# A fixed VectorE order for the opening of the second FFN, and whole residual rows in the projection ahead of it

## The chip, the cores and the metric

The kernel runs on one core of one Trainium2 chip. The time is device microseconds for one execution of the whole two-layer block. Before the change the median of three runs is 2317.76 us (2317.74 to 2318.29).

Engines are named as in the profile: PE is TensorE, DVE is VectorE, ACT is ScalarE, POOL is GpSimd, and SP is SyncE, which here only issues DMAs. Each engine works through its own queue in order, and an instruction that waits holds everything behind it on its engine.

## The reference

The input has 1024 positions of width 1024 in float32, and two layers. Each layer adds a mixer and then an FFN to the residual `h`, both on a normalized `h`:

```
def rms_norm(x, g, eps=EPS):
    xf = x.astype(jnp.float32)
    y = xf * lax.rsqrt(jnp.mean(xf * xf, axis=-1, keepdims=True) + eps)
    return (y * g.astype(jnp.float32)).astype(x.dtype)
...
def conv_ffn(h, w_up, conv_w, conv_b, w_down):
    a, g = jnp.split(h @ w_up, 2, axis=-1)
    a = lax.conv_general_dilated(a, conv_w, window_strides=(1,), padding=((CONV_WIDTH - 1, 0),),
                                 dimension_numbers=('NWC', 'WIO', 'NWC'), feature_group_count=D_FF) + conv_b
    return (jax.nn.gelu(a) * g) @ w_down
...
    for layer in range(DEPTH):
...
        hn = rms_norm(h, norm_mix[layer])
        if layer % 2 == 0:
            mix = even_mixer(...)
        else:
            mix = odd_mixer(...)
        h = h + mix
        h = h + conv_ffn(rms_norm(h, norm_ffn[layer]), ffn_w_up[layer], ...)
    return rms_norm(h, final_norm)
```

The odd mixer of the second layer runs differential attention (six heads) and dilated attention, puts their outputs side by side and projects them with `odd_w_out` back to width 1024. The change lies between the end of that attention and the first products of the second FFN.

## The kernel before

**Numbers and tiles.** Activations lie with the width on the 128 partitions, so `h` is eight row blocks (`kt` 0 to 7) of 128 x 1024, and each row block has two halves of 512 positions. A float32 product is three matmuls: each operand is split into a high part (a cast on ACT, `wh`, `hph`) and the rest (a subtraction on DVE, `wl`, `hpl`), and `mm3` multiplies high by high, high by low and low by high. The eight pairs of blocks `hph`/`hpl` hold the split activations of whatever is projected.

**The end of the odd mixer.** `odd_mixer` runs the heads one after the other. A head is a chain over PE, ACT and DVE: scores (`sc_c`), reductions (`nmx`) and softmax (`pt_c`, `cf`), transposes on PE (`tr_c`) with their copies (`at_c`), products with v (`av_c`), a normalization by small operations on DVE (`ssq`, `rst`), and last a transpose `tr_o` and the result `y`. The output projection is cut in two. `OUT_A` are the six blocks whose input is ready early; it is done inside `odd_mixer` (loop from L1116), eight rows in two halves, 16 products `ps_o1` of 18 matmuls, in two pairs of four rows. Its PSUM tag `mm` has two banks. Each product is added on DVE to a tile `part`, loaded from the residual in DRAM, and stored back (L1123 to L1127), all by SP's queue. `part` is 128 x 512 with two buffers of the tag `sw`. `OUT_B` are the other two blocks, done after the mixer (L1310 on): 16 products `ps_o2` of 6 matmuls.

Which half a product belongs to is seen in its inputs: in the rows of the order below, `hph_0_..` is half 0 and `hph_1_..` half 1. Where a scheduler decides, instructions of the projection are placed between those of the heads, as the buffers, banks and inputs allow. qk0 and qk1 (pool `qk_p`, two buffers each) hold the rotated q and k of a head until they are laid out anew by SP's DMAs (L849).

**The opening of the second FFN.** The class `FFN` serves both layers. For layer 1 the loads of h (L1307) are issued on SP, then for each half eight products `ps_o2`; `add` (L294) adds a product to `h`, squares it on ACT (`nsq`), sums on DVE (`nsum`, L212) and stores h on SP. `ahead` prepares first weights (`wr`, and `a` for the two early columns 2 and 3). `apply` then computes the root by `Norm.stats`: `ps_n` on PE, a chain of twelve small operations on DVE, the copy `n_rb`, and `ps_b` on PE; for half 0 it scales h (`scaled`) and splits it into the blocks b11 and b21 (`put`: cast `hph` on ACT, `hpl` on DVE). Then `up` runs seven products of blocks (`PRODUCTS`) per column of the up projection into `ps_u0` to `ps_u5`; the first two use b11 and b21, and the others need half 1 as well.

```
            for half in range(2):
                for kt in range(KT):
                    ps = ps_acc("ps_o2")
                    proj_T(ps, w, kt * P, half, ncol=S, kts=OUT_B)
                    ff.add(kt, half, ps)
                ff.ahead(half)
            for half in range(2):
                ff.apply(half)
            ff.run(after1)
```

Of the kernel before, what the change touches and what calls it, by code (L numbers as in the profile page):

```python
# [10 lines left out]
F32 = mybir.dt.float32  # L11
F32R = mybir.dt.float32r
# [52 lines left out]
def tile_block(  # L65
# [22 lines left out]
    def pool(name, **kw):  # L88
        return tc.tile_pool(name=name, reuse_waits="tile", **kw)
# [184 lines left out]
    class FFN:  # L274
        def __init__(self, layer, stack):
            self.layer = layer
            hp = stack.enter_context(pool(name=f"ffh{layer}", bufs=1))
# [8 lines left out]
            self.forms = {}  # L286
# [7 lines left out]
        def add(self, kt, half, ps):  # L294
            h = self.hT[kt][half]
            V.tensor_tensor(h, ps, h, op=ALU.add)
# [4 lines left out]
        def apply(self, half):  # L301

            self.scale, _ = self.norm.stats(half * HF)
            if half == 0:
                self.X = self.blocks("x", F32R)
                X = self.X
                self.B = {
                    "b11": ([hph[m][0] for m in range(2)], [hpl[m][0] for m in range(2)]),
                    "b21": ([hph[m + 2][0] for m in range(2)], [hpl[m + 2][0] for m in range(2)]),
                    "b22": ([hph[m + 2][1] for m in range(2)], [hpl[m + 2][1] for m in range(2)]),  # L310
                    "d": ([hph[m][1] for m in range(2)], [hpl[m][1] for m in range(2)]),
                    "e": (X[0], X[1]),
                    "t3": (X[2], X[3]),
                }
                for m in range(4):
                    self.scaled(m, 0)
                    self.put("b11" if m < 2 else "b21", m % 2, self.H[m][0])

        def scaled(self, m, half):
            for kt in (2 * m, 2 * m + 1):  # L320
                t = self.hT[kt][half]
                V.scalar_tensor_tensor(t, t, pcol(PC_FFN[self.layer] + kt), self.scale, op0=ALU.mult, op1=ALU.mult)

        def put(self, name, m, src):
            hi, lo = self.B[name]
# [243 lines left out]
        def up(self):  # L569
# [3 lines left out]
            self.banks += [ps_mx.tile([P, HF], F32, tag="mx", name=f"ps_u{i + 2}") for i in range(4)]  # L573

            both = (0, 1)
            for j in both:
                self.product(j, 1)
                self.product(j, 2)
            for j in both:
                self.forms_of(j, 1)  # L580
                self.block("d", j)
                self.product(self.early[j], 1)
                self.product(self.early[j], 2)
            for j in both:
                self.product(j, 3)
            for j in both:
# [129 lines left out]
    def out_proj(ff):  # L716
        for pair in range(2):
            ws = [get_w(w_eout, pair * 2 + i, "eout") for i in range(2)]
            for half in range(2):
                for i in range(2):  # L720
                    for n in range(2):
                        kt = (pair * 2 + i) * 2 + n
                        ps = ps_acc("ps_o")
                        proj_T(ps, ws[i], n * P, half)
                        ff.add(kt, half, ps)
                    if pair == 1 and half == 1:
                        ff.ahead(i)
                if pair == 1:
                    ff.apply(half)

# [3 lines left out]
    def odd_mixer():  # L734
        stack = ExitStack()
        with stack:
# [378 lines left out]

            for pair in range(2):  # L1116
                ws = [get_w(w_oouta, pair * 2 + i, "oouta", 1536) for i in range(2)]
                for half in range(2):
                    sl = slice(half * HF, (half + 1) * HF)
                    for n in range(4):  # L1120
                        kt = pair * 4 + n
                        part = wk.tile([P, HF], F32, tag="sw", name="part", bufs=2)
                        nc.sync.dma_start(part, h_dram[kt, :, sl])  # L1123
                        ps = ps_mm.tile([P, HF], F32, tag="mm", name="ps_o1")
                        proj_T(ps, ws[n // 2], n % 2 * P, half, kts=OUT_A)
                        V.tensor_tensor(part, ps, part, op=ALU.add)
                        nc.sync.dma_start(h_dram[kt, :, sl], part)  # L1127

# [172 lines left out]
    with ExitStack() as stack:  # L1301
# [7 lines left out]
        for half in range(2):  # L1309
            for kt in range(KT):  # L1310
                ps = ps_acc("ps_o2")
                proj_T(ps, w, kt * P, half, ncol=S, kts=OUT_B)
                ff.add(kt, half, ps)
            ff.ahead(half)
        for half in range(2):
            ff.apply(half)
        ff.run(after1)


# [80 lines left out]
```

## Time and profile before

| | |
|---|---|
| median of three runs | 2317.76 us |
| the profiled execution | 2323.59 us |
| its span | 2321.8 us |
| mean granted clock of PE | 0.994 |
| PE, DVE, ACT, POOL busy in the span | 2257.7, 1670.2, 988.8, 9.4 us |
| first projection (OUT_A) beside heads and alone | 1498.9 to 1613.0 us |
| second projection (OUT_B) | 1613.0 to 1634.7 us |
| first product of the second FFN | 1647.82 us |
| DMA queues in use | SP (q1) and ACT (q10); none of POOL |

Times within the profile count from the start of its span. A row of a group has the line, engine, operation, output and inputs, shapes and count, then busy time, the mean in ns of one, and the idle time just before with what ended it. A row of a window has its bounds, its length, the busy time of each engine with its count, then the granted clock, the share of the DMA engines and what they moved. A row of the timeline has start, duration, engine and line.

### The profile page before, as it was taken

What the parts mean: (1) busy time and instruction counts of PE and PEld (TensorE: products, weight loads), DVE (VectorE), ACT (ScalarE), POOL (GpSimd) and SP (SyncE); (2) the same over time, 40 slices, a digit from 0 to 9 for tenths busy, and PEclk for the clock granted to TensorE, in tenths of its full rate; (3) what the DMA queues carried; (4) which work ended last, traced back from release to release, by engine and by line L of the source; (5) the groups of instructions that cost most, each with busy time, mean ns of one, the idle gap of its engine ahead of it and who ended that gap; (6) DMA issues with size and microseconds to landing.
All of it is one profiled execution on the core that took longest, in us unless ns stands there. A gap on an engine that the chain in (4) does not pass through costs nothing.

```text
span 2321.8 us, 31404 instructions
## 1 busy us (share of the span) xinstructions
PE 2257.7 (97%) x11436; PEld 1900.7 (82%) x11436; DVE 1670.2 (72%) x3267; ACT 988.8 (43%) x1735; POOL 9.4 (0%) x67
## 2 busy tenths in 40 slices
PE   7999999999999999999999999999899999999997
PEld 7888878888887788898988988888678888877787
DVE  6673899787866767545335798886999788766666
ACT  6331355454543333434324445553455454543331
POOL 0000000000000000000000000000000000000000
PEclk9999999999999999999999999999899999999998
DMA  4115135343468663345544253464435343468652
GB/s 136 63 46 200 37 122 195 136 163 136 163 246 288 243 220 132 100 114 131 138 107 120 78 150 97 107 178 137 151 118 199 134 166 136 163 261 295 242 190 73
DMA packets 252155, 354.85 MB, mean 153 GB/s; under 512 B 16736, under 2 KB 172640, under 8 KB 252000
## 3 DMA queue, kind: packets, MB, share of 16 engines
q1 hardware_dynamic: 251136, 351.80, 45.9%
q8 instruction: 90, 1.47, 0.3%
q10 hardware_dynamic: 864, 1.04, 0.2%
q14 instruction: 65, 0.53, 0.1%
HBM read 214.26 MB, written 103.91 MB: 137 GB/s over the span
## 4 chain that ended last, share of the span: by engine, by line
PE 63%; DMA 15%; DVE 15%; ACT 4%; issue 3%; SPq 0%; DVEq 0%; ACTq 0%
PE ps_u L173 9%; PE ps_u L175 9%; PE ps_u L174 9%; DMA wr<-in_w_up 4%; PE ps_qk L175 3%; PE ps_qk L173 3%; PE ps_qk L174 3%; DMA wr<-in_w_dn 2%; DMA hph<-g_dram 2%; DVE wl L376 2%; PE ps_o L173 2%; PE ps_o L174 2%; PE ps_o L175 2%; PE av_c L1041 2%; PE ps_vv L174 2%
## 5 line engine op out<-in xcount | busy, mean ns | idle before, releaser
L173 PE MATMUL ps_u<-hph,wh 128*128 128x512 f32 x960 | 376.3, 393 | 5.8 <-ACT hph L184 2.2
L175 PE MATMUL ps_u<-hph,wl 128*128 128x512 f32 x960 | 374.6, 391 | 0.3 <-DVE wl L376 0.3
L174 PE MATMUL ps_u<-hpl,wh 128*128 128x512 f32 x952 | 371.7, 391 | 0.2 <-DVE hpl L185 0.2
L144 DVE TENSOR_TENSOR wl<-raw,wh 128x1024 fp32r<-128x1024 f32 (+1 forms) x74 | 88.3, 1193 | 196.0 <-ACT wh L143 195.9
L173 PEld LDWEIGHTS ps_u<-hph,wh 128*128 128x128 f32 x960 | 180.6, 188 | 49.2 <-ACT f_s L448 3.4
L175 PEld LDWEIGHTS ps_u<-hph,wl 128*128 128x128 f32 x960 | 180.8, 188 | 39.5 <-DVE wl L376 1.9
L372 ACT CAST wh<-q 128x1024 fp32r<-128x1024 f32 (+1 forms) x136 | 132.8, 976 | 185.1 <-PE ps_u L174 108.2
L174 PEld LDWEIGHTS ps_u<-hpl,wh 128*128 128x128 f32 x952 | 179.4, 188 | 38.1 <-DVE hpl L185 1.3
L376 DVE TENSOR_TENSOR wl<-q,wh 128x1024 fp32r<-128x1024 f32 (+1 forms) x136 | 153.5, 1129 | 42.8 <-ACT wh L372 41.5
L173 PE MATMUL ps_qk<-hph,wh 128*128 128x512 f32 x384 | 152.0, 396 | 0.0
L175 PE MATMUL ps_qk<-hph,wl 128*128 128x512 f32 x384 | 151.3, 394 | 0.0
L174 PE MATMUL ps_qk<-hpl,wh 128*128 128x512 f32 x384 | 151.0, 393 | 0.0
L175 PE MATMUL ps_u<-x,wl 128*128 128x512 f32 x352 | 137.3, 390 | 1.1 <-DVE wl L376 1.1
L174 PE MATMUL ps_u<-x,wh 128*128 128x512 f32 x352 | 137.2, 390 | 1.1 <-DVE x L185 1.1
L173 PE MATMUL ps_u<-x,wh 128*128 128x512 f32 x352 | 137.0, 391 | 0.0
L372 ACT CAST wh<-wr 128x1024 fp32r<-128x1024 f32 (+3 forms) x132 | 100.6, 769 | 68.0 <-PE ps_u L174 34.4
L173 PE MATMUL ps_u<-h,wh 128*128 128x512 f32 x288 | 113.7, 395 | 7.5 <-ACT wh L372 4.0
L143 ACT CAST wh<-raw 128x1024 fp32r<-128x1024 f32 (+1 forms) x74 | 76.0, 1027 | 97.4 <-PE ps_qk L174 34.4
L376 DVE TENSOR_TENSOR wl<-wr,wh 128x1024 fp32r<-128x1024 f32 (+3 forms) x132 | 114.3, 870 | 3.8 <-ACT wh L372 3.6
L174 PE MATMUL ps_u<-h,wh 128*128 128x512 f32 x288 | 112.3, 390 | 1.1 <-DVE h L185 1.1
L175 PE MATMUL ps_u<-h,wl 128*128 128x512 f32 x288 | 112.2, 390 | 0.0
L174 PE MATMUL ps_vv<-wl,hph 128*128 128x256 f32 x384 | 110.0, 286 | 0.0
(276 smaller groups left out, 5262.1 us busy)
## 6 DMA issues: line engine op xcount, KB each, us to landing
wr<-in_w_up SPq DMA_DIRECT2D x88, 512.0 KB, 4.2
g_dram<-stage SPq DMA_DIRECT2D x72, 512.0 KB, 2.6
g_dram<-h SPq DMA_DIRECT2D x70, 512.0 KB, 2.6
hpl<-g_dram SPq DMA_DIRECT2D x48, 512.0 KB, 9.8
hph<-g_dram SPq DMA_DIRECT2D x48, 512.0 KB, 9.6
h<-g_dram SPq DMA_DIRECT2D x42, 512.0 KB, 5.9
wr<-in_w_dn SPq DMA_DIRECT2D x96, 192.0 KB, 2.8
raw<-in_w_oin SPq DMA_DIRECT2D x36, 512.0 KB, 3.8
```

Source lines behind the costliest of these rows:

```text
L143: A.copy(wh, raw)
L144: V.tensor_sub(wl, raw, wh.bitcast(F32))
L173: T.matmul(ps, lh, rh, start=first, stop=False, skip_group_check=more)
L174: T.matmul(ps, lh, rl, start=False, stop=False, skip_group_check=more)
L175: T.matmul(ps, ll, rh, start=False, stop=last, skip_group_check=more)
L372: A.copy(t[0], src)
L376: V.tensor_sub(l, src, h.bitcast(F32))
L1041: T.matmul(av, at, v[:, j, :], start=(j == 0), stop=(j == i))
```

## The change

Four things are done.

1. The residual's first share (OUT_A): the four rows of a pair are loaded as whole rows of 128 x 1024 into tiles `part` that use the tags `qk0` and `qk1`, ahead of the pair's products, on SP. Each half is added in place and stored by POOL's queue. The loops run as before, halves outside, rows inside.
2. The FFN of layer 1 stores h by POOL's queue (`self.queue`), that of layer 0 by SP's still.
3. The opening of the second FFN has a DVE order written by hand (`manual_schedule` for DVE): the eight projections of half 0 with squares, the first of half 1, the early weights and the root of half 0 (`stats(0)`), then the other projections of half 1 with the blocks of half 0 (`first(m)`) between them, then all squares of half 1, and after that `stats(1)`. `apply` is cut into `stats`, `places` and `first`; layer 0 calls them in the old order.
4. In `up` of layer 1, product 1 of the columns 0, 1, 2, 3 comes first and then product 2 of the same. Before, the early columns 2 and 3 came after the block d.

```
         def add(self, kt, half, ps, norm=True):
             h = self.hT[kt][half]
             V.tensor_tensor(h, ps, h, op=ALU.add)
+            if norm:
+                self.square(kt, half)
+
+        def square(self, kt, half):
+            h = self.hT[kt][half]
             self.norm.add(half * HF, kt, h)
-            nc.sync.dma_start(h_dram[kt, :, half * HF : (half + 1) * HF], h)
...
+            self.queue.dma_start(h_dram[kt, :, half * HF : (half + 1) * HF], h)
+        def stats(self, half):
+            self.scale[half], _ = self.norm.stats(half * HF)
+        def first(self, m):
+            self.scaled(m, 0)
+            self.put("b11" if m < 2 else "b21", m % 2, self.H[m][0])
...
-            for j in both:
-                self.product(j, 1)
-                self.product(j, 2)
+            if self.layer:
+                for n in (1, 2):
+                    for j in both + self.early:
+                        self.product(j, n)
...
+                parts = [qk_p.tile([P, S], F32, tag=f"qk{n % 2}", name="part") for n in range(4)]
+                for n, part in enumerate(parts):
+                    nc.sync.dma_start(part, h_dram[pair * 4 + n])
                 for half in range(2):
-                    sl = slice(half * HF, (half + 1) * HF)
-                    for n in range(4):
-                        kt = pair * 4 + n
-                        part = wk.tile([P, HF], F32, tag="sw", name="part", bufs=2)
-                        nc.sync.dma_start(part, h_dram[kt, :, sl])
+                    for n, part in enumerate(parts):
                         ps = ps_mm.tile([P, HF], F32, tag="mm", name="ps_o1")
                         proj_T(ps, ws[n // 2], n % 2 * P, half, kts=OUT_A)
+                        part = part[:, half * HF : (half + 1) * HF]
                         V.tensor_tensor(part, ps, part, op=ALU.add)
-                        nc.sync.dma_start(h_dram[kt, :, sl], part)
+                        G.dma_start(h_dram[pair * 4 + n, :, half * HF : (half + 1) * HF], part)
...
+        ff.places()
+        def project(kt, half, norm=True):
+            ps = ps_acc("ps_o2")
+            proj_T(ps, w, kt * P, half, ncol=S, kts=OUT_B)
+            ff.add(kt, half, ps, norm)
+        with tc.manual_schedule(engines={mybir.EngineType.DVE}):
+            for kt in range(KT):
+                project(kt, 0)
+            project(0, 1, False)
+            ff.ahead(0)
+            ff.stats(0)
+            project(1, 1, False)
+            project(2, 1, False)
+            ff.first(0)
+            project(3, 1, False)
+            ff.first(1)
+            project(4, 1, False)
+            project(5, 1, False)
+            ff.ahead(1)
+            ff.first(2)
+            project(6, 1, False)
+            project(7, 1, False)
+            ff.first(3)
+            for kt in range(KT):
+                ff.square(kt, 1)
+        ff.stats(1)
         ff.run(after1)
```

**PE at the end of the next-to-last head.** In the order's rows `ps_o_14354` is a product `ps_o1` with its number; here the rows of before, at that head's `tr_o`; `ps_o_14400` is the seventh product, the third of half 1:

```order
L173 MATMUL ps_o_14400<-hph_1_83,wh 128x512
L174 MATMUL ps_o_14400<-hpl_1_91,wh 128x512
L175 MATMUL ps_o_14400<-hph_1_83,wl 128x512
L898 MATMUL sc_c<-kl_13829,qs_13825 128x256 x2
L173 MATMUL ps_o_14400<-hph_1_85,wh 128x512
L1054 MATMUL tr_o<-ident,o_sb 128x128 x2
L174 MATMUL ps_o_14400<-hpl_1_93,wh 128x512
L1054 MATMUL tr_o<-ident,o_sb 128x128 x2
```

The same place after the change; `ps_o_14331` is the fourth product, the last of half 0, and `ps_o_14352` the fifth, the first of half 1:

```order
L175 MATMUL ps_o_14331<-hph_0_84,wl 128x512
L1054 MATMUL tr_c<-ident,pt_c 128x128 x7
L1060 MATMUL av_c<-v,at_c 128x128 x7
L1054 MATMUL tr_c<-ident,pt_c 128x128 x8
L1060 MATMUL av_c<-v,at_c 128x128 x8
L916 MATMUL sc_c<-kh_13827,qs_13825 128x256
L916 MATMUL sc_c<-kh_13828,qs_13826 128x256
L917 MATMUL sc_c<-kl_13830,qs_13826 128x256
L916 MATMUL sc_c<-kh_13827,qs_13825 128x256
L1073 MATMUL tr_o<-ident,o_sb 128x128 x4
L173 MATMUL ps_o_14352<-hph_1_89,wh 128x512
```

The matmuls of three half-1 products that stood among the head's transposes and products with v are now behind its `tr_o`. Counted through the whole order, 121 matmuls of `ps_o1` stood ahead of the end of this head and 72 do now; ahead of the last `tr_o` of the last head it was 226 and is 178, of 288.

**DVE at the same place.** After the change, the end of that head's small operations, its result `y`, and the adds of the products `ps_o_14310` and `ps_o_14331`, which are rows 2 and 3 of half 0:

```order
L1069 TENSOR_SCALAR rst<-rst 128x4
L1072 TENSOR_SCALAR o_sb<-o_sb,rst 128x128 x4
L1075 TENSOR_SCALAR y<-tr_o,narrow 128x512
L1146 TENSOR_TENSOR part<-ps_o_14310,part 128x512
L185 TENSOR_TENSOR hpl_1_95<-y,hph_1_87 128x512
L1024 ISA pt_c,nmx<-sc_c,zm 128x128
```

Before, the add of the fifth product (`ps_o_14354`, half 1) stood ahead of that head's small operations, among its copies:

```order
L1037 COPY at_c<-tr_c 128x512
L1009 TENSOR_TENSOR nmx<-nmx 128x1
L1037 COPY at_c<-tr_c 128x384
L1126 TENSOR_TENSOR part<-ps_o_14354,part 128x512
L1016 RECIPROCAL cf<-ssum 128x1
L1017 SCALAR_TENSOR_TENSOR cf<-ssum,narrow,cf 128x1
L1019 SCALAR_TENSOR_TENSOR pt_c<-pt_c,cf 128x1024
```

Two adds that came before the head's end now come behind it.

**DVE in the opening.** After the change, from the end of the root's chain of half 0 (`n_rb`); `h_1_..` are half-1 tiles, `h_0_..` half 0, `ps_b` the broadcast root:

```order
L225 COPY n_rb<-n_y 128x512
L297 TENSOR_TENSOR h_1_14656<-ps_o_14850,h_1_14656 128x512
L297 TENSOR_TENSOR h_1_14658<-ps_o_14858,h_1_14658 128x512
L331 SCALAR_TENSOR_TENSOR h_0_14655<-h_0_14655,narrow,ps_b 128x512 x2
L185 TENSOR_TENSOR hpl_0_90<-h_0_14655,hph_0_82 128x1024
L297 TENSOR_TENSOR h_1_14658<-ps_o_14870,h_1_14658 128x512
L331 SCALAR_TENSOR_TENSOR h_0_14657<-h_0_14657,narrow,ps_b 128x512 x2
L185 TENSOR_TENSOR hpl_0_92<-h_0_14657,hph_0_84 128x1024
L297 TENSOR_TENSOR h_1_14660<-ps_o_14882,h_1_14660 128x512
L297 TENSOR_TENSOR h_1_14660<-ps_o_14890,h_1_14660 128x512
L385 TENSOR_TENSOR wl<-a,wh 128x1024 x2
```

The same place before, where all adds were done by then:

```order
L225 COPY n_rb<-n_y 128x512
L376 TENSOR_TENSOR wl<-wr,wh 128x1024
L376 TENSOR_TENSOR wl<-a,wh 128x1024 x2
L322 SCALAR_TENSOR_TENSOR h_0_14671<-h_0_14671,narrow,ps_b 128x512 x2
L322 SCALAR_TENSOR_TENSOR h_0_14673<-h_0_14673,narrow,ps_b 128x512 x2
L185 TENSOR_TENSOR hpl_0_90<-h_0_14671,hph_0_82 128x1024
L322 SCALAR_TENSOR_TENSOR h_0_14675<-h_0_14675,narrow,ps_b 128x512
```

The adds of half 1 moved behind the root of half 0 and between its blocks, and each of the first two block splits now follows its own scalings directly. On PE `ps_b` of half 0 stands ahead of the last product `ps_o2`, and on ACT the first cast of an early weight `a` ahead of the first cast `hph`.

More of the change, by code (lines that the diff above doesn't have):

```diff
@@ L276, in __init__ @@
             self.layer = layer
+            self.queue = G if layer else nc.sync
             hp = stack.enter_context(pool(name=f"ffh{layer}", bufs=1))
@@ L292, in rows, with add, places @@
             return [[blocks[k // 2][h][:, k % 2, :] for h in range(2)] for k in range(KT)]
-        def add(self, kt, half, ps):
+        def add(self, kt, half, ps, norm=True):
             h = self.hT[kt][half]
             V.tensor_tensor(h, ps, h, op=ALU.add)
+            if norm:
+                self.square(kt, half)
+        def square(self, kt, half):
+            h = self.hT[kt][half]
             self.norm.add(half * HF, kt, h)
-            nc.sync.dma_start(h_dram[kt, :, half * HF : (half + 1) * HF], h)
[L301 to L317, printed above, removed]
+            self.queue.dma_start(h_dram[kt, :, half * HF : (half + 1) * HF], h)
+        def stats(self, half):
+            self.scale[half], _ = self.norm.stats(half * HF)
+        def places(self):
+            self.X = self.blocks("x", F32R)
+            X = self.X
+            self.B = {
+                "b11": ([hph[m][0] for m in range(2)], [hpl[m][0] for m in range(2)]),
+                "b21": ([hph[m + 2][0] for m in range(2)], [hpl[m + 2][0] for m in range(2)]),
+                "b22": ([hph[m + 2][1] for m in range(2)], [hpl[m + 2][1] for m in range(2)]),
+                "d": ([hph[m][1] for m in range(2)], [hpl[m][1] for m in range(2)]),
+                "e": (X[0], X[1]),
+                "t3": (X[2], X[3]),
+            }
+        def first(self, m):
+            self.scaled(m, 0)
+            self.put("b11" if m < 2 else "b21", m % 2, self.H[m][0])
         def scaled(self, m, half):
@@ L321, in scaled @@
                 t = self.hT[kt][half]
-                V.scalar_tensor_tensor(t, t, pcol(PC_FFN[self.layer] + kt), self.scale, op0=ALU.mult, op1=ALU.mult)
+                V.scalar_tensor_tensor(t, t, pcol(PC_FFN[self.layer] + kt), self.scale[half], op0=ALU.mult, op1=ALU.mult)
         def put(self, name, m, src):
@@ L575, in up @@
             both = (0, 1)
-            for j in both:
-                self.product(j, 1)
-                self.product(j, 2)
+            if self.layer:
+                for n in (1, 2):
+                    for j in both + self.early:
+                        self.product(j, n)
+            else:
+                for j in both:
+                    self.product(j, 1)
+                    self.product(j, 2)
             for j in both:
@@ L581, in up @@
                 self.block("d", j)
-                self.product(self.early[j], 1)
-                self.product(self.early[j], 2)
+                if not self.layer:
+                    self.product(self.early[j], 1)
+                    self.product(self.early[j], 2)
             for j in both:
@@ L728, in out_proj @@
                 if pair == 1:
-                    ff.apply(half)
+                    ff.stats(half)
+                    if half == 0:
+                        ff.places()
+                        for m in range(KT // 2):
+                            ff.first(m)
     def odd_mixer():
@@ L1308, in tile_block @@
         w = load_w(w_ooutb)
-        for half in range(2):
-            for kt in range(KT):
[L1311 to L1316, printed above, removed]
+        ff.places()
+        def project(kt, half, norm=True):
[3 more added lines that the diff above has]
+        with tc.manual_schedule(engines={mybir.EngineType.DVE}):
+            for kt in range(KT):
+                project(kt, 0)
[17 more added lines that the diff above has]
+        ff.stats(1)
         ff.run(after1)
```

2 lines of the change are left out of this document (1 added, 1 removed).

## The prediction

> **What bounds the kernel now.** I read the kernel's busy time in stages around the place of the change first, cut at the events that the later views showed: the end of the next-to-last and of the last attention head, the end of each projection, the first product of the second FFN. This is the table by window of the profile of before: length, busy time and count for each engine, then the granted clock and the DMA share.
>
> ```profile
> core 0: us, PE busy (x) PEld busy (x) DVE busy (x) ACT busy (x) POOL busy (x), PEclk, DMA share, GB/s
> 1498.90:1551.80 52.90, 50.35 (x281) 41.82 (x280) 47.33 (x153) 26.65 (x69) 0.00 (x0) 1.00 0.60 166
> 1551.80:1598.40 46.60, 45.95 (x264) 39.11 (x265) 41.10 (x149) 21.32 (x60) 0.00 (x0) 1.00 0.30 103
> 1598.40:1613.00 14.60, 14.60 (x67) 12.13 (x68) 6.23 (x10) 2.73 (x3) 0.13 (x2) 1.00 0.52 163
> 1613.00:1634.70 21.70, 21.70 (x98) 17.96 (x97) 15.46 (x26) 8.21 (x14) 0.00 (x0) 1.00 0.92 319
> 1634.70:1647.80 13.10, 4.50 (x25) 4.33 (x23) 12.73 (x27) 6.87 (x8) 0.00 (x0) 0.59 0.94 314
> 1647.80:1654.00 6.20, 6.03 (x13) 4.30 (x14) 6.20 (x9) 3.14 (x3) 0.00 (x0) 0.50 0.00 0
> 1654.00:1712.00 58.00, 55.90 (x241) 43.50 (x240) 55.68 (x77) 29.83 (x37) 0.20 (x2) 1.00 0.12 34
> ```
>
> Rows 1 and 2 are the last two heads: PE and DVE are both nearly full. Rows 3 and 4 are pure projection, PE alone is full. Row 5 is the hole at the opening of the second FFN. From there to 1712 DVE is full and sets the pace: 55.68 of 58.00. Which work fills PE beside the heads is shown by the same table for the projections' tile alone:
>
> ```profile
> 1498.90:1551.80 52.90, 32.47 (x121) 21.85 (x121) 3.42 (x5) 1.00 0.60 166
> 1551.80:1598.40 46.60, 29.08 (x105) 19.09 (x106) 4.77 (x7) 1.00 0.30 103
> 1598.40:1613.00 14.60, 14.50 (x63) 11.82 (x64) 2.07 (x3) 1.00 0.52 163
> ```
>
> The first projection (OUT_A) has 288 matmuls. 121 of them run beside the next-to-last head, 105 beside the last, and only some 62 stay for the time after. They are filler: while DVE works through a head's scores, PE always has a projection to do.
>
> The hole itself, as PE and DVE record it, with what each engine waited for:
>
> ```profile
> 1634.45 0.39 PE L175 MATMUL ps_o<-hph,wl 128*128 128x512 f32 x1
> 1634.68 0.95 PE L219 MATMUL ps_n<-narrow,nsum 128*128 128x1 f32 x8
> 1642.02 2.08 PE L228 MATMUL ps_b<-ident,n_rb 128*128 128x128 f32 x8 [6.40 <-DVE n_rb L225]
> 1647.82 1.22 PE L173 MATMUL ps_u<-hph,wh 128*128 128x512 f32 x2 [2.22 <-ACT hph L184]
> ```
>
> ```profile
> 1614.11 0.69 DVE L1126 TENSOR_TENSOR part<-ps_o,part 128x512 f32<-128x512 f32 x1 [4.38 <-DMA part<-h_dram]
> 1619.72 0.69 DVE L296 TENSOR_TENSOR h<-ps_o,h 128x512 f32<-128x512 f32 x1 [4.92 <-DMA h<-h_dram]
> ```
>
> PE's last projection matmul is at 1634.45, its first product at 1647.82. DVE began late, at 1619.72, held by a load, and had a backlog when PE was through.
>
> **The opening.** The durations, by form, from 1613 to 1660 (count, busy time, mean of one in ns, then what ended the idle time before them):
>
> ```profile
> L296 DVE TENSOR_TENSOR h<-ps_o,h 128x512 f32<-128x512 f32 x16 | 10.7, 681 | 5.1 <-DMA h<-h_dram 5.1
> L212 DVE TENSOR_TENSOR nsum<-nsum,nsq 128x512 f32<-128x512 f32 x14 | 9.5, 680 | 0.1
> L185 DVE TENSOR_TENSOR hpl<-h,hph 128x1024 fp32r<-128x1024 f32 x4 | 4.8, 1214 | 0.0
> L376 DVE TENSOR_TENSOR wl<-wr,wh 128x1024 fp32r<-128x1024 f32 x2 | 2.4, 1222 | 0.0
> L184 ACT CAST hph<-h 128x1024 fp32r<-128x1024 f32 x4 | 4.2, 1045 | 6.2 <-DVE h L322 6.2
> ```
>
> And two steps of the root's chain with its last copy, in DVE's order of time:
>
> ```profile
> 1639.34 0.16 DVE L193 TENSOR_TENSOR rs_t<-n_y 128x4 f32<-128x4 f32 x1
> 1639.54 0.16 DVE L194 SCALAR_TENSOR_TENSOR rs_t<-rs_t,n_v 128x4 f32<-128x4 f32 x1
> 1641.54 0.43 DVE L225 COPY n_rb<-n_y 128x512 f32<-128x512 f32 x1
> ```
>
> What it may bring: no arithmetic goes, so DVE's 89 us of work from 1619.72 to 1712 stay, and a gain can only be an earlier start (4.92, the wait for the load) and DVE's own pauses (64.20 less 61.88, row 6 and 7 together, 2.3). That is at most 7.2.
>
> What it does to DVE's queue: PE needs 21.70 for sixteen products, 1.36 each; add and square sum take two pitches of about 0.60, so in the first half DVE now keeps up and waits for PE. Compare the backlog when PE is through. Before, two adds, four sums, the root's chain with n_rb, four weight splits, eight scalings, four block splits. After, by the fixed order, some six adds and eight sums, but two weight splits and no chain. The difference is four or five adds and four sums more (5.2), two splits (2.3) and the chain with the copy (2.8) less: nothing. The early start is used up in waiting for PE.
>
> What it adds are waits with nothing beside them, because the order is fixed and one DVE instruction holds all behind it:
> - PE stands at ps_b in its own order, ahead of the last ps_o2, until the chain of twelve dependent small operations at a pitch of 0.20 (1639.34 to 1639.54) and n_rb (0.43) are done: 2.8, less the product beside it (1.36): 1.4.
> - The splits of blocks 0 and 1 directly follow their two scalings, and each waits for ACT's cast of 1.045: twice 1.1. Before, two to four scalings stood between. The first cast stands on ACT behind a weight cast that waits for the last ps_o2: up to 1.0 more. Adds stand behind these splits, and PE's ps_u0 and ps_u1 wait for those adds' banks.
> - The half-1 root now comes after all squares. ps_n and ps_b stand on PE ahead of the next products, and DVE's next scaling waits for ps_b, whose 2.08 were at the half clock of row 5: about 1.2 with the way there and back. The casts of the combined weights queue behind eight squares on ACT: about 1.0.
>
> The early products ps_u2 and ps_u3, now ahead of the d blocks, fill some of PE's hole, but DVE is the bound there, so I give them nothing.
>
> Sum 1.4 + 2.2 + 1.0 + 1.2 + 1.0 = 6.8, of which I take 6. The bounds are −7.2 (all of the above gain and none of the waits) and +9.
>
> **The residual's first share.** Before, each half row had a tile of its own, loaded just ahead. Now four whole rows of a pair live in the two buffers each of qk0 and qk1. The last head still needs one of each until SP has sent its relayout (L849); the last row is the end of the next-to-last head on PE:
>
> ```profile
> 1533.91 0.50 SPq L849 DMA_DIRECT2D qs<-qs  x1
> 1534.46 0.59 SPq L849 DMA_DIRECT2D qs<-qk  x1
> 1536.84 0.46 SPq L849 DMA_DIRECT2D qs<-qk  x1
> 1544.27 0.46 SPq L849 DMA_DIRECT2D kl<-kl  x1
> 1551.82 0.43 PE L1054 MATMUL tr_o<-ident,o_sb 128*128 128x128 f32 x2 [0.43 <-DVE o_sb L1053]
> ```
>
> And what a transfer of this size takes from issue to landing (the DMA issues from 1495 to 1650):
>
> ```profile
> part<-h_dram SPq DMA_DIRECT2D x16, 256.0 KB, 3.1
> h_dram<-part SPq DMA_DIRECT2D x16, 256.0 KB, 2.1
> h<-h_dram SPq DMA_DIRECT2D x16, 256.0 KB, 5.3
> h_dram<-h SPq DMA_DIRECT2D x16, 256.0 KB, 5.3
> ```
>
> So rows 2 and 3 of the first pair are loaded at about 1542 to 1545 instead of ahead. Their adds (ps_o_14310, ps_o_14331) stand on DVE behind the head's last operation y, and these two products hold both PSUM banks of the tag until then. So no half-1 product can start beside the next-to-last head. The order shows it: before tr_o of that head PE had 121 projection matmuls, as in the trace, and has 72 now; beside the last head 105 before, 106 now. 62 were left after the heads, 110 are left now. They run where PE alone is the bound: 48 x 0.2267 (1613.00 to 1634.70, 21.70 over 96) = **10.9 us**. That costs in full if the heads end when they did, and nothing if PE set their pace. DVE is busy 47.33 of 52.90 there and loses three adds and two weight splits to later, some 3.7. The chain of scores, reductions, transposes and copies stays. I let the heads end 1.5 earlier, so this term is **+9.4**, with bounds 0 and 10.9.
>
> The stores' move to GpSimd's queue: no DMA issue of that engine is in the trace, so its price is bounded by SP's 256 KB stores, 2.1 here and 5.3 later in the crowded opening, and by nothing from below; I take 2.1, the nearest. Pair 1's loads wait for pair 0's stores, with 20 us to spare. SP drops 32 stores, so the weights' loads are no longer behind the h stores; that is in the opening's term. The third load of y moves ahead of the last head's relayout on SP; PE's whole idle time beside the next-to-last head is 52.90 less 50.35, and what this takes off it I do not count.
>
> **Sum.** 2323.59 (the profiled execution) + 9.4 + 6 = 2339.0. That execution was 5.83 over the median of 2317.76, so 2333 on the scale of the runs.
>
> **Rivals.**
> 1. *PE sets the pace in both places* (faster). Then 48 matmuls fewer let the heads end 10.9 sooner and the first term is 0, and in the opening the filled hole counts up to DVE's 7.2: 2311. It decides once the heads end 8 sooner than now. For it: PE is at 45.95 of 46.60 beside the last head. Against: DVE is at 47.33 of 52.90 beside the one before, in dependent steps, and from 1654 on DVE, not PE, has no pause.
> 2. *A draw*. Half of the filler is made good by earlier heads (10.9 / 2, +5), and the opening keeps 5 of its 7.2 because ACT's casts come in time: 2318. For it: ACT is busy 26.65 of 52.90 and 21.32 of 46.60 only; against it stands the order of ACT and DVE in the opening.
> 3. *GpSimd's stores come late* (slower still). The half-1 loads of h wait for pair 1's stores, rows 1 and 3 for the last ones. A store of 5.3 and a load of 5.3 after the last add put them about 11 after it, where the first half-1 add is due 11 to 12 after; it decides from there on. Twice that store time makes every half-1 add about 5 late; with the upper ends of the other terms, 10.9 and 9: 2343. [...]
> 4. *The whole rows do not hold banks*, if loads of rows 2 and 3 came early enough. The order speaks against it; it is the 0 of that term.
>
> **Chances.** Forecast 2333 (2323 to 2341): 0.60. Rival 1, with 4: 0.13. Rival 2: 0.13. Rival 3: 0.14. About 0.2% (4.6 us) is what a measurement of this kernel can tell from no change. Faster 0.13, same 0.13, slower 0.74. The range leaves out the ends of rivals 1 and 3: 2313 to 2344.
>
> **What would show it.** PE's count of projection matmuls ahead of the heads' last tr_o (some 178, not 226) and the heads' end near 1597; pauses of PE for DVE between the third product and y; the first ps_u some 2 us after the last ps_o2 instead of 13.4, and DVE with some 8 us of pauses before 1720 for ACT's hph and wh. I am wrong if the heads end 8 or more earlier, or if the opening's DVE stays gapless.

## The result: 22.5 us slower, and the profile after

| | before | after |
|---|---|---|
| median of four runs | 2318.03 us (2317.74 to 2319.61) | 2340.54 us (2339.22 to 2343.01) |
| the profiled execution, its span | 2323.59, 2321.8 us | 2339.7, 2337.9 us |
| mean granted clock of PE | 0.994 | 0.992 |
| PE, DVE, ACT, POOL busy in the span | 2257.7, 1670.2, 988.8, 9.4 us | 2260.5, 1673.4, 990.0, 26.8 us |

The ratio is 1.0096 with a 95% interval of 1.0084 to 1.0107. The work of PE, DVE and ACT has hardly changed; POOL now issues the stores. So most of the time went into waiting.

Both profiles agree in work up to the third head from the end, but that head's `tr_o` is at 1487.7 before and at 1484.9 after: before's profiled execution was 2.8 behind already ahead of the change. I therefore measure two stages from there: from this `tr_o` to PE's last matmul of the first projection (1613.0 and 1622.2), and on to the same add of `ps_u` into `f_s` behind the first columns (L462 before, L471 after; 1714.87 and 1731.44). **The first stage takes 125.3 before and 137.3 after (+12.0), the second 101.9 and 109.2 (+7.4).** Together that is 19.4; the medians differ by 22.5. The other 3.1 I cannot place: one profiled execution of before stood 5.6 over its median.

The table by window of the kernel after: the next-to-last head, the last one, pure projection, and the opening.

```profile
1496.00:1546.20 50.20, 40.88 (x231) 34.19 (x229) 44.07 (x148) 25.49 (x67) 1.23 (x2) 0.96 0.51 147
1546.20:1596.60 50.40, 48.67 (x266) 41.05 (x266) 42.94 (x150) 23.22 (x62) 3.78 (x7) 0.93 0.41 136
1596.60:1622.20 25.60, 25.54 (x114) 21.18 (x115) 8.41 (x13) 3.81 (x5) 3.23 (x6) 1.00 0.48 150
1622.20:1731.44 109.24, 92.49 (x386) 72.02 (x385) 94.56 (x139) 47.58 (x61) 9.52 (x21) 0.92 0.29 102
```

And the projections' tile alone in the first three of these windows:

```profile
1496.00:1546.20 50.20, 19.57 (x72) 13.11 (x72) 1.36 (x2) 0.96 0.51 147
1546.20:1596.60 50.40, 30.26 (x106) 19.85 (x106) 4.78 (x7) 0.93 0.41 136
1596.60:1622.20 25.60, 25.14 (x110) 20.82 (x111) 4.13 (x6) 1.00 0.48 150
```

The reader is to see three things. Beside the next-to-last head PE has 72 projection matmuls, not 121, and is busy for 40.88 of 50.20, no longer 50.35 of 52.90. So 110 are left for the time when PE runs alone, not 62, and that time is 25.60, not 14.60. And the granted clock of the two heads is 0.96 and 0.93, where before it was 1.00.

What PE waited for there, from its timeline after:

```profile
1535.33 2.84 PE L1060 MATMUL av_c<-v,at_c 128*128 128x128 f32 x14 [2.06 <-DVE nmx L1028]
...
1546.20 1.09 PE L1073 MATMUL tr_o<-ident,o_sb 128*128 128x128 f32 x4 [3.33 <-DVE o_sb L1072]
...
1548.72 0.79 PE L173 MATMUL ps_o<-hph,wh 128*128 128x512 f32 x1 [1.44 <-DVE part L1146]
```

PE now stands idle through the chain that ends the head. The third row shows the hold: the next projection waits for the add of `part` on DVE, which frees its bank. SP's timeline shows why that add is late:

```profile
1538.89 0.53 SPq L1140 DMA_DIRECT2D part<-h_dram  x1
1540.56 0.46 SPq L868 DMA_DIRECT2D kl<-kl  x1
1541.07 0.58 SPq L1140 DMA_DIRECT2D part<-h_dram  x1
```

The loads of the whole rows 2 and 3 are issued at the end of the head's relayout (L868, L849 before), which they have to wait for.

**The opening.** DVE's waits by line and by what ended them, over the second stage without its last 16 us, before and then after:

```profile
DVE h L296 <- DMA h<-h_dram: 5.1, 2, 4.9
DVE part L1126 <- DMA part<-h_dram: 4.4, 1, 4.4
DVE wl L376 <- ACT wh L372: 1.8, 2, 1.1
DVE f_s L454 <- PE ps_u L175: 0.2, 1, 0.2
```

```profile
DVE nsum L212 <- ACT nsq L211: 5.2, 7, 0.8
DVE part L1146 <- PE ps_o L175: 3.4, 1, 3.4
DVE hpl L185 <- ACT hph L184: 2.3, 2, 1.2
DVE h L331 <- PE ps_b L228: 2.2, 1, 2.2
DVE f_s L463 <- PE ps_u L175: 1.7, 1, 1.7
DVE h L297 <- PE ps_o L175: 1.3, 2, 0.7
DVE wl L385 <- ACT wh L381: 0.6, 1, 0.6
```

(Columns: total, times, longest. The `part` rows belong for the most part to the time before the window.) Before, DVE waited for loads, once, and then hardly at all. After, no load is waited for, and in its place stand seven waits for ACT's square, two for the cast `hph`, one for the second root. DVE's work in the whole second stage is 92.94 before and 94.56 after; its idle time is 101.87 less 92.94, 8.9, and 109.24 less 94.56, 14.7. Idle time makes 5.8 of the 7.4.

PE's side of it after:

```profile
1645.09 1.16 PE L228 MATMUL ps_b<-ident,n_rb 128*128 128x128 f32 x8 [1.38 <-DVE n_rb L225]
...
1648.88 0.50 PE L173 MATMUL ps_u<-hph,wh 128*128 128x512 f32 x1 [1.26 <-ACT hph L184]
...
1654.99 0.80 PE L173 MATMUL ps_u<-hph,wh 128*128 128x512 f32 x1 [3.46 <-DVE h L297]
```

The hole of 13.4 that before had between its last projection and its first product is gone from this place: the last projection matmul is at 1647.23 and the first product at 1648.88. But PE's idle time in the second stage has grown, from 10.9 (101.87 less 91.00) to 16.8 (109.24 less 92.49), since a hole has opened at the second root:

```profile
1673.79 1.02 PE L219 MATMUL ps_n<-narrow,nsum 128*128 128x1 f32 x8 [1.36 <-DVE nsum L212]
1679.20 2.05 PE L228 MATMUL ps_b<-ident,n_rb 128*128 128x128 f32 x8 [4.39 <-DVE n_rb L225]
```

Before, `ps_n` of the second root stood inside the first hole, at 1643.89, and its `ps_b` came at 1664.85 without a wait. Every kernel with the new opening waits at this place, 4.4 to 5.4 for `ps_b`; before, e2 and e8 do not.

### The profile page after: what moved, and what is told of

Its sections match the earlier page's. It is cut to its first block, busy times and chain, and to the rows that moved or that the text cites. A ratio compares the mean times of both kernels' runs of the same rounds, so it can differ in the third digit from the quotient of the medians.

```text
span 2337.9 us, 31408 instructions
## 1 busy us (share of the span) xinstructions
PE 2260.5 (97%) x11436; PEld 1902.6 (81%) x11436; DVE 1673.4 (72%) x3267; ACT 990.0 (42%) x1735; POOL 26.8 (1%) x99
## 4 chain that ended last, share of the span: by engine, by line
PE 82%; DVE 8%; DMA 7%; ACT 1%; issue 1%; SPq 0%; DVEq 0%; ACTq 0%
PE ps_u L173 15%; PE ps_u L175 15%; PE ps_u L174 15%; PE ps_qk L175 3%; PE ps_qk L173 3%; PE ps_qk L174 3%; DMA hph<-g_dram 2%; DMA wr<-in_w_dn 2%; PE ps_o L173 2%; PE ps_o L174 2%; PE ps_o L175 2%; PE ps_vv L173 2%; PE ps_vv L174 2%; PE ps_vv L175 2%; PE av_c L1060 2%
```

## The experiments

Each is compared with the kernel before, measured beside it (medians 2319.09 for e1 to e4, 2318.69 for e5 to e8, 2319.33 for e9 to e11, 2318.99 for e12). The two stages of each, measured as above, lead through them. "Waits" is DVE's idle time in the second stage (its length less DVE's busy time by the table by window); the last two columns are the sum of the two stages against before, and the difference of the medians.

| kernel | first stage | second stage | DVE busy | waits | stages | medians |
|---|---|---|---|---|---|---|
| before | 125.3 | 101.9 | 92.9 | 8.9 | | |
| after | 137.3 | 109.2 | 94.6 | 14.7 | +19.4 | +22.5 |
| e1 opening alone | 124.4 | 120.2 | 94.7 | 25.4 | +17.4 | +20.3 |
| e2 whole rows alone | 139.6 | 101.0 | 93.5 | 7.5 | +13.4 | +12.8 |
| e3 after, rows mixed | 125.7 | 115.4 | 94.6 | 20.7 | +13.9 | +14.5 |
| e4 after, stores on SP | 140.1 | 115.1 | 94.5 | 20.5 | +28.0 | +27.1 |
| e5 after, sums later | 138.4 | 108.8 | 94.7 | 14.1 | +20.0 | +21.2 |
| e6 after, interleaved | 138.7 | 104.5 | 93.9 | 10.6 | +16.1 | +15.8 |
| e7 after, no fixed order | 138.2 | 105.6 | 93.0 | 12.6 | +16.6 | +17.5 |
| e8 before, part stores on GpSimd | 124.8 | 99.5 | 93.7 | 5.8 | −2.9 | −0.8 |
| e9 opening alone, part stores on GpSimd | 124.5 | 117.8 | 94.7 | 23.0 | +15.1 | +15.8 |
| e10 e9, interleaved | 124.1 | 112.7 | 93.5 | 19.2 | +9.6 | +12.3 |
| e11 after, old order of products | 137.8 | 111.7 | 95.9 | 15.8 | +22.3 | +23.6 |
| e12 e10, weights loaded earlier | 124.8 | 110.7 | 93.7 | 17.0 | +8.4 | +10.7 |

The two stages explain every kernel to within 3.1 us. The first stage has two values, about 125 and 137 to 140, and what decides is one thing: whether rows 2 and 3 of the first pair are whole rows. In the second, DVE's work is the same to within 3 us and the waits are what differs.

**Part by part (e1, e2).** e1 is the changed kernel with the first projection's residual as before (half rows, stores on SP); e2 is the kernel before with only the whole rows and their stores on GpSimd:

```
e1:
-                parts = [qk_p.tile([P, S], F32, tag=f"qk{n % 2}", name="part") for n in range(4)]
+                        part = wk.tile([P, HF], F32, tag="sw", name="part", bufs=2)
+                        nc.sync.dma_start(part, h_dram[kt, :, sl])
...
-                        G.dma_start(h_dram[pair * 4 + n, :, half * HF : (half + 1) * HF], part)
+                        nc.sync.dma_start(h_dram[kt, :, sl], part)
```

> The residual's first share is put back as it was (half-row tiles, SP's stores); the opening with its fixed order, the products' order and the h stores by GpSimd stay. Theory A (two losses: about 12 to 15 us beside the heads by held banks, about 6 to 8 in the opening): 2324 to 2327 us, heads' end and OUT_A's end as before. Rival B (all of the loss comes from the whole rows, the opening is neutral or a gain): 2318 us or below. Rival C (all of the loss is the opening): 2340 us.

> Before with the whole residual rows and GpSimd's stores of them alone. Theory A: 2330 to 2333 us, 178 of 288 first-projection matmuls ahead of the last head's end and 110 behind it. Rival B: 2340 us. Rival C: 2318 us. If the two parts are independent, this loss and that of the opening alone add up to 22 us.

e1: 2339.39 us (ratio 1.0086, interval 1.0071 to 1.0101). e2: 2331.89 us (1.0055, 1.004 to 1.007). The rows are as expected, +12.8. The opening alone is a miss: +20.3, where I had expected some 6. The two parts make 33.1 apart and 22.5 together, so each takes some of the other's loss. DVE's waits of e1 in the opening name what is dear:

```profile
DVE wl L385 <- ACT wh L381: 5.3, 3, 3.0
DVE h L297 <- DMA h<-h_dram: 5.2, 2, 4.5
DVE nsum L212 <- ACT nsq L211: 5.2, 7, 0.8
DVE part L1146 <- DMA part<-h_dram: 4.2, 1, 4.2
DVE h L331 <- PE ps_b L228: 3.2, 2, 2.2
DVE hpl L185 <- ACT hph L184: 2.6, 2, 1.5
...
```

The waits for loads of before are there again, and the new waits of the fixed order come on top; and the first weights' split `wl`, which the order puts ahead of the root, waits for its cast and that for a load (in e9, where this split waits 5.5, ACT's two casts wait 1.59 and 2.69 for the loads of `wr`).

**The bank hold (e3).** Rows 2 and 3 of the first pair get half-row tiles again; all else stays as in the changed kernel:

```
-                parts = [qk_p.tile([P, S], F32, tag=f"qk{n % 2}", name="part") for n in range(4)]
+                parts = [qk_p.tile([P, S], F32, tag=f"qk{n % 2}", name="part") for n in range(4 if pair else 2)]
...
+                            part = wk.tile([P, HF], F32, tag="sw", name="part", bufs=2)
+                            nc.sync.dma_start(part, h_dram[pair * 4 + n, :, sl])
```

> The changed kernel, but in the first pair only rows 0 and 1 are whole rows in qk0 and qk1; rows 2 and 3 use half-row tiles of the old tag, loaded just ahead. Stores by GpSimd and the second pair stay as changed. Theory A (the banks are held because rows 2 and 3 are loaded only after the last head's relayout): the loss beside the heads goes, 2324 to 2328 us, 221 matmuls ahead of the last head's end. Rival (whole rows or GpSimd's stores as such cost the time): 2340 us, unchanged.

2333.63 us (1.0061, 1.0046 to 1.0076): 14.5 over before, where the changed kernel is 22.5 over. The first stage is that of before again. The table by window of this kernel, for the stretch up to the end of the next-to-last head, the last head and the rest of the projection:

```profile
1485.40:1549.50 64.10, 61.12 (x332) 51.10 (x333) 53.57 (x170) 30.99 (x77) 3.40 (x6) 1.00 0.61 176
1549.50:1595.40 45.90, 45.16 (x262) 38.37 (x261) 39.98 (x144) 21.34 (x58) 2.75 (x6) 1.00 0.37 132
1595.40:1611.08 15.68, 15.68 (x72) 13.03 (x72) 6.36 (x10) 3.81 (x5) 2.18 (x4) 1.00 0.64 202
```

The last head takes 45.90 at a clock of 1.00 (after: 50.40 at 0.93) and 15.68 are left (25.60). That shows the bank hold, and that the slower last head comes with it. The time is above the expected range all the same, since of the 11.6 that the first stage gains the opening gives 6.1 back: its waits rise from 14.7 to 20.7, 5.3 of it for loads of h.

**GpSimd's stores (e4, e8).** e4 is the changed kernel with all stores on SP. e8 is the kernel before with only the stores of `part` on GpSimd:

```
e4:
-            self.queue = G if layer else nc.sync
+            self.queue = nc.sync
...
-                        G.dma_start(h_dram[pair * 4 + n, :, half * HF : (half + 1) * HF], part)
+                        nc.sync.dma_start(h_dram[pair * 4 + n, :, half * HF : (half + 1) * HF], part)
e8:
-                        nc.sync.dma_start(h_dram[kt, :, sl], part)
+                        G.dma_start(h_dram[kt, :, sl], part)
```

> The changed kernel with all its stores on SP's queue again. Theory A: GpSimd's queue costs nothing on the path; 2338 to 2343 us, the same as the changed kernel, or a few us slower where SP's queue holds loads behind stores. Rival D (GpSimd's stores are late and delay the loads of h or slow VectorE): faster than the changed kernel by 4 us or more, 2336 us or below.

> The kernel before with only the stores of the residual's first share on GpSimd's queue. If SP's stores delayed the loads of h (4.92 us wait of VectorE at the opening): 2314 to 2317 us, 1 to 4 us faster than before, with 227 first-projection matmuls ahead of the last head's end as before. Rival: the loads wait for the stores' data whichever queue issues them; 2318 to 2320 us, the same as before.

e4: 2346.22 us (1.0114, 1.0097 to 1.0131): 27.1 over before, 4.6 more than the changed kernel; its executions (2344.70 to 2348.74) lie above all of that kernel's. A row of waits that the kernel after does not have is there again:

```profile
...
DVE h L297 <- DMA h<-h_dram: 4.7, 2, 4.5
...
```

In e4 the last add of `part` is done at 1626.58, and its store stands on SP ahead of the loads of h; after, where GpSimd stores, these loads begin at 1617.00. The kernel before has the same order on SP and shows the hold: its last add of `part` is done at 1614.80, SP's last two stores of `part` last from 1611.02 to 1615.14, and the loads of h begin at 1615.19. So a store that waits for its add holds the loads behind it. e8: 2317.9 us (0.9994, 0.9985 to 1.0003), no change that can be measured, though its opening waits fell from 8.9 to 5.8. So the stores are no loss, and what gains from them is the fixed order: 4.6 here, and 4.5 beside half rows (e9 against e1, below), where the kernel before gains nothing that can be measured.

**The fixed order (e5, e6, e7).** e5 lets each sum come one product later, so that ACT's square is done. e6 does that too, puts scalings and adds between a block's scaling and its split, the early weights later and two squares of half 1 earlier. e7 leaves DVE's order to the scheduler.

```
e5:
             for kt in range(KT):
-                project(kt, 0)
-            project(0, 1, False)
+                project(kt, 0, False)
+                if kt:
+                    ff.square(kt - 1, 0)
+            project(0, 1, False)
+            ff.square(KT - 1, 0)
e6, beside that:
-            ff.first(0)
-            project(3, 1, False)
-            ff.first(1)
+            ff.scaled(0, 0)
+            project(3, 1, False)
+            ff.scaled(1, 0)
+            put(0)
...
+            ff.ahead(1)
+            ff.square(0, 1)
+            ff.square(1, 1)
+            put(3)
e7:
-        with tc.manual_schedule(engines={mybir.EngineType.DVE}):
+        if True:
```

> The changed kernel with one thing moved in the fixed order: in half 0 the square sum of row k comes behind the add of row k+1 instead of directly behind its own. Theory S (each sum waits 0.70 to 0.76 us for ACT's square with nothing between, seven times, and VectorE sets the pace there at 2.05 us a product): 3 to 5 us less than the changed kernel, 2336 to 2338 us, and no wait of the sums for ACT in the profile. Rival H (PE sets the pace there and covers these waits): 2340 us, unchanged.

> As the one before, and in the fixed order each block's split stands behind an add or the next block's scaling instead of directly behind its own scalings; the early weights are prepared after the blocks, and two half-1 squares come ahead of the last split. Theory S: the splits' two waits of 1.1 us for ACT and the cast held by the early weights go as well; 4 to 7 us less than the skewed order alone, 2330 to 2333 us. Rival H: unchanged against the skewed order.

> The changed kernel, with the same calls in the same program order but VectorE left to the scheduler. Theory S (it is the fixed order that puts waits on VectorE): 5 to 9 us less, 2332 to 2336 us; the loss beside the heads stays. Rival Q (the opening costs by its sequence: root of half 0 early, half-1 squares late): 2339 to 2342 us, unchanged.

e5: 2339.87 us (1.009, 1.0075 to 1.0105), as slow as the changed kernel. The sums' seven waits went, and other waits came: DVE's waits of e5 in the opening, without the one for `part`:

```profile
...
DVE h L331 <- PE ps_b L228: 2.9, 2, 2.2
DVE hpl L185 <- ACT hph L184: 2.2, 2, 1.1
DVE f_s L463 <- PE ps_u L175: 2.1, 1, 2.1
DVE h L297 <- PE ps_o L175: 2.0, 3, 0.7
DVE n_v L222 <- PE ps_n L219: 1.8, 1, 1.8
DVE wl L385 <- ACT wh L381: 1.0, 1, 1.0
...
```

Beside whole rows PE sets the pace while it projects: in the kernel after, its only pauses over 0.8 us from 1622 to the first product are 1.38 and 1.26. What DVE saves by then it spends waiting for PE: for `ps_o` and, new, for `ps_n`. e6: 2334.53 us (1.0069, 1.0054 to 1.0084), 6.7 less over before than the changed kernel; the splits' waits for `hph` are gone from its list, and PE's wait of 3.46 with them. That is 1.5 over the range of theory S, but far from unchanged. e7: 2336.23 us (1.0072, 1.0056 to 1.0089), 5.0 less, at the upper edge of its theory S. So the fixed order as written is worse than the scheduler's order of the same work and than a better fixed one, by 5 to 7 us. Neither comes back to the 101.0 that the second stage takes in e2 with its old opening: e6 stays 3.5 above it and e7 4.6. Both still have the hole at the second root, which e2 has not: PE waits 4.99 and 5.37 for the root there, and behind it DVE waits 2.4 and 1.8 for `ps_u`, in e2 0.2. How much of the rest this makes was not tested.

**The order of products (e11).** In the up projection of layer 1 the two early columns come after the block d again:

```
-            if self.layer:
-                for n in (1, 2):
-                    for j in both + self.early:
-                        self.product(j, n)
-            else:
-                for j in both:
-                    self.product(j, 1)
-                    self.product(j, 2)
+            for j in both:
+                self.product(j, 1)
+                self.product(j, 2)
```

> The changed kernel with only the product order of the up projection put back (columns 0 and 1, then the block d, then the early columns). Theory A (the order of products is worth nothing, DVE is the bound there): 2338.5 to 2342.5. Rival P (the early products' four banks hold PE ahead of d and cost time): 2330 to 2336. Rival F (they fill PE's hole and save): 2344 to 2350.

2342.9 us (1.01, 1.0085 to 1.0116), 0.4 over the edge of the first theory: 23.6 over before, against 22.5. The intervals of the two overlap almost wholly, so this part is worth nothing that can be measured, though the second stage of its one profile is 2.5 longer.

**Why the opening is dearer beside half rows (e9, e10, e12).** e9 is e1 with the stores of `part` on GpSimd, e10 is that with the order of e6, and e12 loads the first weights earlier:

```
e12, beside e10:
         for half in range(2):
             for kt in range(KT):
                 nc.sync.dma_start(ff.hT[kt][half], h_dram[kt, :, half * HF : (half + 1) * HF])
+            if half == 0:
+                ff.raw(0)
+                ff.raw(1)
```

> The changed kernel, but the first projection's residual in half-row tiles as before (loaded on SP just ahead of each product), with their stores on GpSimd. Theory Q (with half rows and their stores on SP, the fixed opening cost 20.3 because SP, in order, held the loads of h and of the first weights behind 16 stores; the order itself costs what it cost beside whole rows, about 6 to 10): 2325 to 2330. Rival T (the order alone is the price, whatever the stores): 2336 to 2341. By Q the first addition of the opening waits under 1.5 us for its load, and ps_b of half 0 under 3 for n_rb (7.69 with the stores on SP).

> The kernel of the run before it, with the opening's order changed as in the interleaved run: sums one product behind, the block splits behind other work, early weights earlier, two half-1 squares ahead of the rest. Theory Q: the 5 to 6 that this order took off the changed kernel come off here too, 2320 to 2325, so that what stays over before is the root and splits of half 1, about 3. Rival T: the order's gain was only possible because of the late start behind whole rows, 2326 to 2331.

e9: 2335.16 us (1.0069, 1.0056 to 1.0081), between the two expectations. SP's stores were 4.5 of e1's 20.3, and the first additions wait 0.47 for their load, as theory Q had it; but `ps_b` still comes 7.55 late, against it, as PE's timeline of e9 has it:

```profile
1639.00 2.08 PE L228 MATMUL ps_b<-ident,n_rb 128*128 128x128 f32 x8 [7.55 <-DVE n_rb L225]
```

e10: 2331.63 us (1.0052, 1.004 to 1.0065): the better order gains 3.5 here and not 5 to 6, just outside rival T's range. DVE's waits of e10 show what it waits for instead:

```profile
DVE wl L385 <- ACT wh L381: 10.8, 3, 8.7
DVE part L1146 <- DMA part<-h_dram: 6.0, 1, 6.0
DVE h L331 <- PE ps_b L228: 3.2, 2, 2.2
...
```

The waits of e9 for squares (5.2) and casts `hph` (2.6) are gone, and the wait at `wl` has grown from 5.5 to 10.8. SP's timelines show where its weights come from, e10 first and then the kernel after:

```profile
1606.27 12.09 SPq L1327 DMA_DIRECT2D h<-h_dram  x16
...
1618.82 10.93 SPq L367 DMA_DIRECT2D wr<-in_w_up  x4
```

```profile
1588.79 10.13 SPq L367 DMA_DIRECT2D wr<-in_w_up  x4
...
1617.00 14.85 SPq L1327 DMA_DIRECT2D h<-h_dram  x16
```

Beside half rows SP issues the weights behind all loads of h; beside whole rows they are issued beside the last head, 28 us ahead of them. Why they are placed so differently I did not test. With the same fixed opening the second stage is longer by 18.3 beside half rows (e9's less e8's) and by 8.3 beside whole rows (after's less e2's).

> The interleaved opening beside half rows (the run e10), with one thing more: the first weights wr of the columns 0 and 1, which that run loaded behind all sixteen loads of h, are loaded between the eight of half 0 and the eight of half 1. Theory L (what the fixed order lost beside half rows is VectorE standing at the weight splits that come ahead of the root, 10.8 in that run, because SP loads those weights last): these waits fall under 1.5, VectorE's idle time in the opening from 19.2 to about 9, and the time is 2319 to 2324. Rival H (the four loads push the loads of half 1 back by some 6, and the additions of half 1 wait instead): the waits for wr go and waits for h come, 2327 to 2332. Rival R (the order's own waits, for the casts and for both roots, carry the loss): 2327 to 2332 without new waits for h.

e12: 2329.65 us (1.005, 1.0037 to 1.0064). Rival H holds. DVE's waits of e12:

```profile
...
DVE nsum L212 <- ACT nsq L211: 4.7, 1, 4.7
DVE h L297 <- DMA h<-h_dram: 4.3, 1, 4.3
...
DVE wl L385 <- ACT wh L381: 0.3, 1, 0.3
```

10.8 at `wl` became 0.3, and 9.0 came back, 4.3 at h and 4.7 at one sum, whose square stood on ACT behind the cast of a weight that had not landed (ACT waits 5.06 for it). So moving one load only moves the wait: beside half rows the opening comes before the loads of h and of the weights have all landed, and the fixed order waits for each of them in turn. No run has all of them loaded in time, so that this is the whole of the difference between 18.3 and 8.3 is argued, not shown. No version that ran beats the kernel before; e8 equals it.

## Why the prediction was right, step by step, and where it was not

- **Direction and mechanism: right.** Both terms were forecast as losses, in these two places, and both were. The time lies 7.5 over the forecast and only 0.5 under the upper end of the range. 12.0 and 7.4 stand against the forecast's 9.4 and 6; the other 3.1 of the 22.5 no stage shows.
- **The bank hold: right, and shown.** 72 and 106 matmuls beside the last two heads and 110 after them are the numbers that the order gave (178 ahead of the last `tr_o`). e3 takes the hold away and has the old stage again, which refutes rival 4. (Three adds moved behind the end of the next-to-last head, 5 of them beside it before and 2 after, as the prediction has it; the section on the change counts two.)
- **The size of that term: off, 12.0 in place of 9.4,** and over the upper bound of 10.9. The step that failed is "I let the heads end 1.5 earlier". The 48 displaced matmuls did cost 25.60 less 14.60, 11.0. But the heads ended 1.1 later against the common start (1596.7 less 1484.9 is 111.8, 1598.4 less 1487.7 is 110.7). The next-to-last head gained 2.8, as supposed (61.3 in place of 64.1). The last one lost 3.9 (50.5 in place of 46.6), which no term had. (21.70 over 96 is 0.226 and not 0.2267; the 10.9 stands.)
- **The opening: the size nearly right (7.4 in place of 6), part of the composition wrong.** Right were the wait at `ps_b` (1.38, forecast 1.4), the two splits behind ACT's casts (1.18 and 1.11, forecast 1.1 each), the adds behind them holding PE's products (3.46), and the first product 1.65 after the last projection matmul (forecast some 2). Wrong was "DVE now keeps up and waits for PE". In the first half DVE waited for ACT's squares, 5.2 in all, because the fixed order asks for each sum right behind its own add; two pitches of 0.60 left out this wait. That the early start is used up was right all the same: e5 takes the squares' waits away, and PE's take their place. So the size came out near in part by luck: of the "some 8 us" of pauses that I laid to `hph` and `wh`, only 2.9 are theirs (2.3 and 0.6), and the squares' 5.2 stand in their place.
- **The second root: mis-sized.** 1.2 was forecast; DVE waits 2.2 for `ps_b` there, and 1.7 more for `ps_u` behind it. PE's hole of 4.39 at this place stands in no term.
- **GpSimd's stores: right that they cost nothing; the sum gave them no gain of their own.** e4 puts that gain at 4.6. Rival 3 is refuted: no half-1 add after waits for its load. No run shows the doubled store time in its sum, twice 5.3: GpSimd's stores of `part` took a median of 2.4 from issue to landing (SP's 2.1 before) and those of h 2.5 (SP's 5.3).
- **Rivals 1 and 2: refuted.** PE did not set the heads' pace: with 49 matmuls fewer beside it the next-to-last head ended 2.8 sooner, where 8 was the point from which it decides. The draw needed earlier heads and ACT's casts in time; the heads ended 1.1 later, and the casts were late.
- **What the sum hid:** it adds two terms as if they were independent. The opening's 6 was right beside whole rows (7.4 over before, 8.3 over e2) and would have been far too small for the opening alone (18.3). Beside whole rows the loads of h and of the first weights are in time for the fixed order: in the kernel after, DVE waits for none of them.

## What to carry to other kernels

A fixed order on one engine has to be laid out against when its inputs land, DMAs and other engines' casts included, and it holds only for the surroundings in which it was laid out: the same opening cost 8 or 18 us. Filler that kept PE busy beside a latency-bound chain was worth here what its loss added to the time for which PE later ran alone, 11.0 us for 48 matmuls; a buffer shared with that chain took it away through the two PSUM banks, 121 matmuls beside the head becoming 72. And the hole of 13.4 that closed on PE, where DVE set the pace, gained nothing: another opened at the second root, and PE's idle time rose from 10.9 to 16.8. So count the idle time of the engine that sets the pace, over the whole stage.

## What the hardware showed that I had not expected

PE's pauses beside the next-to-last head came with a lower clock. The granted clock is 0.96 over the window that ends with the pause of 3.33 us at `tr_o` and 0.93 over the last head behind it; in before and in e3, whose longest pauses of PE in these two heads are 1.58 and 1.41, it is 1.00 in both. In finer windows of the kernel after it is 0.50 from 1535.86 to 1539.27, behind the pause of 2.06, and from 1546.10 to 1552.93, behind the pause of 3.33; in between and from there to the end of the last head it is 1.00.

The last head took 3.9 longer, all of it in its first half, where the clock is low (28.4 in place of 23.8; the second half 22.0 in place of 22.8). At the granted 0.50, 6.83 us hold 3.4 less of PE's work. So taking filler away from PE came with two costs, the displaced work and a slower last head. That the clock makes this head slower is argued and not shown: DVE also has more to do beside it (42.9 in place of 41.1), and no run has the one without the other. What sets a drop off is not shown either: one came behind a pause of 2.06 and one behind a pause of 3.33, and no run changes the pauses alone.

The four issues of the first weights' loads, 512 KB each, took SP 0.55 to 3.02 us apiece in the kernel before, where they stand behind sixteen loads of h and eight stores. Beside the last head in the kernel after, the same issues took 0.54 to 0.67 each. In e10, right behind sixteen loads of h, the four take 10.93 us from the start of the first to the end of the fourth. So what an issue cost SP here did not go by its size alone, and it was dearest in the crowded opening; what makes the difference no run separates.
